# PEER gates on one Trainium2 core: a weight split in two parts, compares with one operand in PSUM, accumulators that hold their banks

## The chip, the cores and the metric

The kernel runs on one core of a Trainium2 chip. The metric is device time in microseconds; the median of three executions of the kernel before is 3694.65 us (3694.28 to 3696.64). The engines are PE (TensorE, matmuls; PEld is its weight load), DVE (VectorE), ACT (ScalarE), POOL (GpSimd) and SP (SyncE, which issues most transfers).

## The reference

Two model blocks run over 256 tokens of width 2048. The change touches only the PEER feed-forward part of the first block: eight heads pick 16 experts each out of 16384, by two lists of 128 keys.

```python
s1, i1 = lax.top_k(s[..., 0, :], PEER_TOPK)
s2, i2 = lax.top_k(s[..., 1, :], PEER_TOPK)
cand = s1[..., :, None] + s2[..., None, :]          # 16 x 16 per head
top_s, pos = lax.top_k(cand, PEER_TOPK)             # eid = i1 * 128 + i2
gate = jax.nn.softmax(top_s, axis=-1)
act = gelu(einsum('nd,nhkd->nhk', hx, expert_u[e]))
return einsum('nhk,nhkd->nd', gate * act, expert_v[e])
```

The kernel does not gather experts. It computes the activation of every expert for every token (up pass), a dense matrix of gates that is zero for experts not chosen, and multiplies the product of both into expert_v (down pass).

## The kernel before

float32 products are made from two float32r parts: a high part (a cast on ACT, L140) and a low part (x minus high, a subtraction on DVE or POOL, L142). `K.split` issues both. float32r operands take one matmul record; products of plain float32 operands take two.

**The up pass** (`Peer.up`, L1171) runs over 128 blocks of 128 experts. For a block it loads 1 MB of peer_u (tile `raw`, two buffers), transposes it with two DVE instructions (L1184, tile `tr`, four buffers), splits it in halves (tiles `hi` and `lo`, three buffers each) and issues 16 pairs of matmuls: 512 columns with the high part (L1203) and 256 columns with the low part (L1204). The block's accumulator `gu` is one PSUM bank from a pool of six that go round. Eviction is an ACT copy (L239), a DVE add (L241, tile `act`) and a Gelu on ACT (L1212).

**The side work** is put between the blocks. `Peer.route` (L1047) finds the 128 chosen pairs of keys for half of the tokens: maxima, sums of candidates (L1073), and a lookup by compare (L1099), multiply (L1101) and sum (L1103), all on DVE. `Peer.gates` (L1124) then builds the dense gates, four tokens at a time. The 128 choices of a token lie on the partitions. `factors` makes two matrices for each token: o2, one-hot in the second key (L1136, one compare of 512 elements for four tokens), and o1, one-hot in the first key times the weight. o1 comes from ACT by two activations (L1142, L1143: the square of the distance, then Relu of w minus w times that square) or from DVE by a tensor_scalar (L1145). GATE_ACT says for how many of the four tokens ACT does it: four in the first half of the tokens, two in the second. `product` multiplies the two by an fp32 matmul of 128 columns for each token (L1152) into a bank `psg`, and `store` copies the bank to SBUF on ACT (L1158).

**The order.** `UP_PLAN` (L30) gives the rate: 40 blocks beside the first half's route, 50 blocks beside the second half's route and the first half's gates in turn, 32 blocks beside the second half's gates; the last 6 blocks have no side work. From the 90th block on (`UP_FREE`, L31) DVE computes one of four low parts in every block, before that in every second block. Inside the block a scheduler (L2042) fixes the order of the instructions on each engine when the program is built. Engines work through their queues in that order.

Of the kernel before, what the change touches and what calls it, by code (L numbers as in the profile page):

```python
# [9 lines left out]
F32 = mybir.dt.float32  # L10
F32R = mybir.dt.float32r
# [3 lines left out]
AF = mybir.ActivationFunctionType  # L15
ALU = mybir.AluOpType
# [4 lines left out]
T = 256  # L21
# [10 lines left out]
GATE_ACT = (4, 2)  # L32
# [961 lines left out]
class Peer:  # L994
    def __init__(self, k, hn2, pool, h_d):
        self.k, self.hn2, self.pool, self.tr, self.h_d = k, hn2, pool, pool, h_d
        self.anchor = {}
        self.pI = [pool.tile([128, T], F32, name=f"pI{i}") for i in range(3)]
        self.ni1, self.nw = (pool.tile([128, T], F32, name=f"pN{i}") for i in range(2))
        self.iota = pool.tile([128, 128], F32, name="iota")  # L1000
        k.nc.gpsimd.iota(self.iota, pattern=[[1, 128]], base=0, channel_multiplier=0,
                         allow_small_or_imprecise_dtypes=True)
# [44 lines left out]
    def route(self, pool, tt):  # L1047

        k, nc, a = self.k, self.k.nc, self.k.a
# [3 lines left out]
        it16 = self.iota[:, 0:16]  # L1053
        sv = W("sv", [128, 16, 16])
# [11 lines left out]
        P.tensor_copy(sif, si)  # L1066
        tv = W("tv", [128, 8, 16])
# [3 lines left out]
        def sums(h):  # L1071
            cds[h] = W("cd", [128, 16, 16], 2)
            V.tensor_tensor(cds[h], sv[:, 2 * h, :, None].to_broadcast([128, 16, 16]),  # L1073
                            sv[:, 2 * h + 1, None, :].to_broadcast([128, 16, 16]), op=ALU.add)
# [41 lines left out]
        for i in range(3):  # L1116
            V.tensor_copy(self.pI[i][:, tt * 128:(tt + 1) * 128], ps[:, i * 128:(i + 1) * 128])
        for dst, i in ((self.ni1, 0), (self.nw, 2)):
            V.tensor_scalar(dst[:, tt * 128:(tt + 1) * 128], ps[:, i * 128:(i + 1) * 128], -1.0, None, op0=ALU.mult)
# [4 lines left out]
    def gates(self, tt, scr, g_d, act):  # L1124


        k, nc = self.k, self.k.nc
        i1, i2, w = self.pI
# [3 lines left out]
        key = self.iota[:, None, :].to_broadcast([128, 4, 128])  # L1132

        def factors(t0):
            o2 = self.pool.tile([128, 4, 128], F32, tag="oh2", bufs=3, name="oh2")
            nc.vector.tensor_tensor(o2, key, tok(i2, t0), op=ALU.is_equal)  # L1136
            o1 = self.pool.tile([128, 4, 128], F32, tag="oh1", bufs=3, name="oh1")
            for j in range(4):
                t = t0 + j
                if j < act:  # L1140

                    S.activation(o1[:, j], self.iota, AF.Square, bias=self.ni1[:, t:t + 1])  # L1142
                    S.activation(o1[:, j], o1[:, j], AF.Relu, scale=self.nw[:, t:t + 1], bias=w[:, t:t + 1])  # L1143
                else:
                    nc.vector.tensor_scalar(o1[:, j], self.iota, i1[:, t:t + 1], w[:, t:t + 1], op0=ALU.is_equal,  # L1145
                                            op1=ALU.mult)
            return t0, o2, o1

        def product(t0, o2, o1):
            ps = k.bank("psg")  # L1150
            for j in range(4):
                nc.tensor.matmul(ps[:, j * 128:(j + 1) * 128], lhsT=o2[:, j], rhs=o1[:, j], start=True, stop=True)  # L1152
            return t0, ps
# [10 lines left out]
        for t0 in range(128 * tt, 128 * tt + 136, 4):  # L1164
# [4 lines left out]
            yield  # L1169

    def up(self, act_d):  # L1171
# [24 lines left out]
        def back():  # L1196
            n, c, hi, lo = ready.pop(0)
            if c == 0:
                self.ps = k.gp.tile([128, 512], F32, tag="g", name="gu")
            ps = self.ps  # L1200
# [108 lines left out]
def peer(k, x2, xq, norm, hh, h_d, g_d, act_d, acts, es, finish):  # L1309
# [11 lines left out]
    with tc.tile_pool(name="up", bufs=1) as up:  # L1321
        pe.pool = up
        main = pe.up(act_d)
        route = [pe.route(up, tt) for tt in range(2)]
        gates = [pe.gates(tt, two, g_d, act) for tt, act in enumerate(GATE_ACT)]
# [754 lines left out]
```

## Time and profile before

| | us |
|---|---|
| median of three executions | 3694.65 |
| the profiled execution | 3696.7 |
| its span | 3694.9 |
| PE busy in the span | 3570.3 (97%) |
| DVE busy | 2617.8 (71%) |
| ACT busy | 2030.2 (55%) |
| POOL busy | 1323.9 (36%) |

The up pass lies between about 999 and 1836 us. Gate products stand between 1253.8 and 1790.2 us. Shares over the whole span say little about it, since stages with other limits are in them; the stretches of the pass are read one by one below. Busy time of PE is modelled and overlaps; the distance between the starts of two matmuls says more than their durations.

### The profile page before, as it was taken

The page shows a single profiled execution, that of the slowest core. Times are in us where ns is not written, and L with a number is a line of the kernel's source. Part 1 is how long each engine was busy: PE and PEld are TensorE (multiplying, and loading weights), DVE is VectorE, ACT ScalarE, POOL GpSimd, SP SyncE. Part 2 cuts the span into 40 slices and gives each one's busy share as a digit, 9 for nine tenths or more (in the row PEclk, how much of TensorE's full clock was granted, in tenths as well). Part 3 has the DMA queues.
Part 4 walks back from the last instruction along what each step waited for, and adds up shares of the span by engine and source line. Part 5 has one row for each costly group of instructions (what it writes and reads, how often), then busy time and mean ns, then how long its engine had stood idle before and what let it go on. Part 6 is the DMA issues. An engine that isn't in the chain of part 4 may idle for free.

```text
span 3694.9 us, 55970 instructions
## 1 busy us (share of the span) xinstructions
PE 3570.3 (97%) x19751; PEld 2991.5 (81%) x19751; DVE 2617.8 (71%) x4165; ACT 2030.2 (55%) x3861; POOL 1323.9 (36%) x1339
## 2 busy tenths in 40 slices
PE   9999999999999999998899999999999999989998
PEld 7678888878888888887788888888788887878777
DVE  5766777667588888788644444446899879667766
ACT  5555556545454677766544444445555667444674
POOL 1333223211288777755511111111234544142001
PEclk9999999999999999999999999999999999999999
DMA  7444434477698888878977777765554445645434
GB/s 221 138 160 129 131 122 132 140 230 244 172 204 207 201 213 221 219 180 208 253 246 237 229 235 231 221 200 187 164 172 145 141 139 171 192 145 184 144 120 149
DMA packets 377277, 681.21 MB, mean 184 GB/s; under 512 B 44493, under 2 KB 128373, under 8 KB 375845
## 3 DMA queue, kind: packets, MB, share of 16 engines
q1 hardware_dynamic: 343104, 625.05, 58.0%
q10 hardware_dynamic: 33893, 52.58, 4.2%
q8 instruction: 156, 2.56, 0.3%
q14 instruction: 124, 1.02, 0.1%
HBM read 627.57 MB, written 47.22 MB: 183 GB/s over the span
## 4 chain that ended last, share of the span: by engine, by line
PE 45%; DVE 3%; ACT 1%; DMA 1%; issue 1%; POOL 0%; SPq 0%; ACTq 0%; DVEq 0%; POOLq 0%
PE g L205 13%; PE g L207 7%; PE gv L1250 5%; PE gv L1251 5%; PE gv L1252 5%; PE dv L1252 2%; PE dv L1250 2%; PE dv L1251 2%; DVE lo L142 1%; PE g L229 1%; PE g L228 1%; PE g L230 1%; ACT hi L140 1%; PE psl L1840 1%; DMA raw<-in_peer_u_dram 1%
## 5 line engine op out<-in xcount | busy, mean ns | idle before, releaser
L142 DVE TENSOR_TENSOR lo<-raw,hi 128x1024 fp32r<-128x1024 f32 (+3 forms) x856 | 1039.3, 1218 | 622.6 <-ACT hi L140 618.7
L140 ACT CAST hi<-raw 128x1024 fp32r<-128x1024 f32 (+3 forms) x858 | 867.3, 1013 | 908.3 <-PE gv L1252 395.8
L205 PE MATMUL g<-x,hi 128*128 128x512 f32 x3040 | 1091.2, 401 | 13.0 <-DVE x L1662 9.0
L207 PE MATMUL g<-x,lo 128*128 128x256 f32 x3040 | 844.0, 288 | 16.7 <-DVE lo L142 16.5
L1203 PE MATMUL gu<-x,hi 128*128 128x512 f32 x2048 | 733.0, 398 | 1.7 <-ACT hi L140 1.7
L142 POOL TENSOR_TENSOR lo<-tr,hi 128x512 fp32r<-128x512 f32 x429 | 589.2, 1401 | 250.8 <-ACT hi L140 175.2
L205 PEld LDWEIGHTS g<-x,hi 128*128 128x128 f32 x3040 | 568.3, 189 | 133.0 <-issue 19.8
L207 PEld LDWEIGHTS g<-x,lo 128*128 128x128 f32 x3040 | 575.0, 189 | 53.0 <-DVE lo L142 26.9
L1204 PE MATMUL gu<-x,lo 128*128 128x256 f32 x2048 | 580.2, 284 | 30.4 <-POOL lo L142 27.3
L1203 PEld LDWEIGHTS gu<-x,hi 128*128 128x128 f32 x2048 | 386.4, 189 | 88.6 <-ACT hi L140 2.4
L1204 PEld LDWEIGHTS gu<-x,lo 128*128 128x128 f32 x2048 | 386.7, 189 | 48.5 <-POOL lo L142 44.7
L1184 DVE STREAM_TRANSPOSE tr<-raw 128x1024 f32<-128x1024 f32 x256 | 309.0, 1231 | 90.6 <-POOL lo L142 43.8
L140 ACT CAST hi<-tr 128x512 fp32r<-128x512 f32 x512 | 290.0, 616 | 76.2 <-PE gu L1203 54.5
L142 POOL TENSOR_TENSOR g<-scr,g 128x512 fp32r<-128x512 f32 x64 | 114.9, 1797 | 572.0 <-ACT g L140 572.0
L1252 PE MATMUL gv<-hi,g 128*128 128x512 f32 x756 | 299.7, 396 | 0.0
L1251 PE MATMUL gv<-lo,g 128*128 128x512 f32 x756 | 299.7, 396 | 0.0
L1250 PE MATMUL gv<-hi,g 128*128 128x512 f32 x756 | 238.4, 396 | 0.0
L1212 ACT ACTIVATE act<-act 128x256 f32<-128x256 f32 x128 | 53.4, 417 | 222.6 <-DVE act L241 222.3
L205 PE MATMUL g<-y2m,hi 128*128 128x512 f32 x512 | 175.2, 397 | 0.3 <-ACT hi L140 0.3
L1251 PEld LDWEIGHTS gv<-lo,g 128*128 128x128 f32 x756 | 142.4, 188 | 34.7
L1252 PEld LDWEIGHTS gv<-hi,g 128*128 128x128 f32 x756 | 142.4, 188 | 34.7
L1250 PEld LDWEIGHTS gv<-hi,g 128*128 128x128 f32 x756 | 142.4, 188 | 34.7
(604 smaller groups left out, 5856.4 us busy)
## 6 DMA issues: line engine op xcount, KB each, us to landing
raw<-in_peer_u_dram SPq DMA_DIRECT2D x512, 256.0 KB
raw<-in_peer_v_dram SPq DMA_DIRECT2D x256, 512.0 KB
raw<-in_a_w_in_dram SPq DMA_DIRECT2D x160, 512.0 KB
raw<-in_w_in_dram SPq DMA_DIRECT2D x136, 512.0 KB
raw<-in_b_w_in_dram SPq DMA_DIRECT2D x64, 512.0 KB
raw<-in_a_w_out_dram SPq DMA_DIRECT2D x48, 512.0 KB
raw<-in_w_out_dram SPq DMA_DIRECT2D x32, 512.0 KB
raw<-in_w_peer_query_dram SPq DMA_DIRECT2D x32, 512.0 KB
```

The source lines that it names most:

```text
L140: ins = nc.scalar.copy(hi, x) if heng == "act" else nc.vector.tensor_copy(hi, x)
L142: return ins, eng.tensor_tensor(lo, x, hi.bitcast(F32), op=ALU.subtract)
L205: nc.tensor.matmul(ps[f], lhsT=hi[:, k, f * 128:(f + 1) * 128], rhs=x2[:, q, :], start=(q == 0), stop=False)
L207: nc.tensor.matmul(ps[f][:, 0:T], lhsT=lo[:, k, f * 128:(f + 1) * 128], rhs=x2[:, q, 0:T], start=False, stop=(q == nk - 1))
L228: nc.tensor.matmul(ps[tt], lhsT=x, rhs=w, start=(q == 0), stop=False)
L1184: st["t"] = nc.vector.transpose(tr.rearrange("p b (u j) -> p u b j", u=2), raw[:, 2 * u:2 * u + 2].rearrange("p u (b j) -> p u b j", j=32))
L1203: nc.tensor.matmul(ps, lhsT=hi[:, j], rhs=self.hn2[:, q, :], start=(q == 0), stop=False)
L1204: st["m"] = nc.tensor.matmul(ps[:, 0:T], lhsT=lo[:, j], rhs=self.hn2[:, q, 0:T], start=False, stop=(q == KT - 1))
L1212: nc.scalar.activation(o, o, AF.Gelu)
L1250: nc.tensor.matmul(p, lhsT=x, rhs=hi, start=first, stop=False)
L1251: nc.tensor.matmul(p, lhsT=x, rhs=lo, start=False, stop=False)
L1252: nc.tensor.matmul(p, lhsT=g2[:, T + tt * 128:T + tt * 128 + 128], rhs=hi, start=False, stop=last)
```

## The change

`gates` no longer uses ACT for o1. Each token's weight is split into a high and a low float32r part (`pw`, made once for each half by `K.split`), and one scalar_tensor_tensor on DVE makes both parts of o1 for a token: 256 elements, the compare of the key with i1, times the two weights. o2 and o1 are float32r tiles, and each token takes two matmuls of 128 columns, one for each part, that accumulate. The key list iota is copied into a PSUM bank, and sv and sif (the route's values and indices) are copied into PSUM as well, so that the compares and the route's three operations read one operand from PSUM and one from SBUF. `banks` takes all six banks of the pool for the whole pass: four accumulators that go round by block number, one bank for iota and sif, one for sv.

```diff
--- before.py
+++ after.py
@@ -29,7 +29,6 @@
 LAST = [(1536, 2), (1792, 2)]
 UP_PLAN = (40, 50, 32)
 UP_FREE = 90
-GATE_ACT = (4, 2)
 DECAY_C = math.exp(-0.5)
 HALVES = [slice(0, 64), slice(64, 128)]
 QUAD = "(a b i)"
@@ -995,8 +994,8 @@
     def __init__(self, k, hn2, pool, h_d):
         self.k, self.hn2, self.pool, self.tr, self.h_d = k, hn2, pool, pool, h_d
         self.anchor = {}
-        self.pI = [pool.tile([128, T], F32, name=f"pI{i}") for i in range(3)]
-        self.ni1, self.nw = (pool.tile([128, T], F32, name=f"pN{i}") for i in range(2))
+        self.pI = [pool.tile([128, T], F32, name=f"pI{i}") for i in range(2)]
+        self.pw = pool.tile([128, 2, T], F32R, name="pw")
         self.iota = pool.tile([128, 128], F32, name="iota")
         k.nc.gpsimd.iota(self.iota, pattern=[[1, 128]], base=0, channel_multiplier=0,
                          allow_small_or_imprecise_dtypes=True)
@@ -1050,7 +1049,7 @@
         V, S, P, E = nc.vector, nc.scalar, nc.gpsimd, nc.tensor
         s = self.s
         W = lambda n, shape, bufs=1, dt=F32, p=pool: p.tile(shape, dt, tag="w_" + n, bufs=bufs, name=n)
-        it16 = self.iota[:, 0:16]
+        it16 = self.iotaP[:, 0:16]
         sv = W("sv", [128, 16, 16])
         si = W("si", [128, 16, 16], dt=U32)
         for j in range(16):
@@ -1064,13 +1063,16 @@
                 yield
         sif = W("sif", [128, 16, 16])
         P.tensor_copy(sif, si)
+        S.copy(self.sifP, sif)
+        S.copy(self.svP, sv)
+        sif, svP = self.sifP, self.svP
         tv = W("tv", [128, 8, 16])
         ti = W("ti", [128, 8, 16], dt=U32)
         cds = {}
 
         def sums(h):
             cds[h] = W("cd", [128, 16, 16], 2)
-            V.tensor_tensor(cds[h], sv[:, 2 * h, :, None].to_broadcast([128, 16, 16]),
+            V.tensor_tensor(cds[h], svP[:, 2 * h, :, None].to_broadcast([128, 16, 16]),
                             sv[:, 2 * h + 1, None, :].to_broadcast([128, 16, 16]), op=ALU.add)
 
         sums(0)
@@ -1113,43 +1115,39 @@
         ps = k.bank("psr")
         for i in range(3):
             E.transpose(ps[:, i * 128:(i + 1) * 128], res[:, i].rearrange("p h j -> p (h j)"), k.ident)
-        for i in range(3):
-            V.tensor_copy(self.pI[i][:, tt * 128:(tt + 1) * 128], ps[:, i * 128:(i + 1) * 128])
-        for dst, i in ((self.ni1, 0), (self.nw, 2)):
-            V.tensor_scalar(dst[:, tt * 128:(tt + 1) * 128], ps[:, i * 128:(i + 1) * 128], -1.0, None, op0=ALU.mult)
+        ts = slice(tt * 128, (tt + 1) * 128)
+        for i in range(2):
+            V.tensor_copy(self.pI[i][:, ts], ps[:, i * 128:(i + 1) * 128])
+        k.split(ps[:, 256:384], self.pw[:, 0, ts], self.pw[:, 1, ts])
         yield
 
     GATE_TOK = 32
 
-    def gates(self, tt, scr, g_d, act):
-
+    def gates(self, tt, scr, g_d):
 
         k, nc = self.k, self.k.nc
-        i1, i2, w = self.pI
+        (i1, i2), w = self.pI, self.pw.bitcast(F32)
         S = nc.scalar
         n = self.GATE_TOK
         tok = lambda x, t: x[:, t:t + 4, None].to_broadcast([128, 4, 128])
-        key = self.iota[:, None, :].to_broadcast([128, 4, 128])
+        key = lambda n: self.iotaP[:, None, :].to_broadcast([128, n, 128])
 
         def factors(t0):
-            o2 = self.pool.tile([128, 4, 128], F32, tag="oh2", bufs=3, name="oh2")
-            nc.vector.tensor_tensor(o2, key, tok(i2, t0), op=ALU.is_equal)
-            o1 = self.pool.tile([128, 4, 128], F32, tag="oh1", bufs=3, name="oh1")
+            o2 = self.pool.tile([128, 4, 128], F32R, tag="oh2", bufs=3, name="oh2")
+            nc.vector.tensor_tensor(o2, key(4), tok(i2, t0), op=ALU.is_equal)
+            o1 = self.pool.tile([128, 4, 2, 128], F32R, tag="oh1", bufs=3, name="oh1")
             for j in range(4):
                 t = t0 + j
-                if j < act:
-
-                    S.activation(o1[:, j], self.iota, AF.Square, bias=self.ni1[:, t:t + 1])
-                    S.activation(o1[:, j], o1[:, j], AF.Relu, scale=self.nw[:, t:t + 1], bias=w[:, t:t + 1])
-                else:
-                    nc.vector.tensor_scalar(o1[:, j], self.iota, i1[:, t:t + 1], w[:, t:t + 1], op0=ALU.is_equal,
-                                            op1=ALU.mult)
+                nc.vector.scalar_tensor_tensor(o1[:, j], key(2), i1[:, t:t + 1], w[:, :, t:t + 1].to_broadcast([128, 2, 128]),
+                                               op0=ALU.is_equal, op1=ALU.mult)
             return t0, o2, o1
 
         def product(t0, o2, o1):
             ps = k.bank("psg")
             for j in range(4):
-                nc.tensor.matmul(ps[:, j * 128:(j + 1) * 128], lhsT=o2[:, j], rhs=o1[:, j], start=True, stop=True)
+                for u in range(2):
+                    nc.tensor.matmul(ps[:, j * 128:(j + 1) * 128], lhsT=o2[:, j], rhs=o1[:, j, u], start=(u == 0),
+                                     stop=(u == 1))
             return t0, ps
 
         def store(t0, ps):
@@ -1167,6 +1165,15 @@
             done = product(*made) if made else None
             made = factors(t0) if t0 < 128 * tt + 128 else None
             yield
+
+    def banks(self):
+
+
+        b = [self.k.gp.tile([128, 512], F32, tag="g", name="gu") for _ in range(6)]
+        self.acc = b[0:4]
+        self.iotaP = b[4][:, 0:128]
+        self.sifP, self.svP = (x.rearrange("p (j i) -> p j i", j=16) for x in (b[4][:, 256:512], b[5][:, 0:256]))
+        self.k.nc.scalar.copy(self.iotaP, self.iota)
 
     def up(self, act_d):
 
@@ -1195,9 +1202,7 @@
 
         def back():
             n, c, hi, lo = ready.pop(0)
-            if c == 0:
-                self.ps = k.gp.tile([128, 512], F32, tag="g", name="gu")
-            ps = self.ps
+            ps = self.acc[n % 4]
             for j in range(8):
                 q = c * 8 + j
                 nc.tensor.matmul(ps, lhsT=hi[:, j], rhs=self.hn2[:, q, :], start=(q == 0), stop=False)
@@ -1320,9 +1325,10 @@
     two = scr.rearrange("p (a b) f -> p a (b f)", a=2)
     with tc.tile_pool(name="up", bufs=1) as up:
         pe.pool = up
+        pe.banks()
         main = pe.up(act_d)
         route = [pe.route(up, tt) for tt in range(2)]
-        gates = [pe.gates(tt, two, g_d, act) for tt, act in enumerate(GATE_ACT)]
+        gates = [pe.gates(tt, two, g_d) for tt in range(2)]
         side = pe.anchored(itertools.chain(route[0], alternate(route[1], gates[0]), gates[1]))
         R, G, due = pe.ROUTE_STEPS, 34, 0.0
         rates = [R / UP_PLAN[0]] * UP_PLAN[0] + [(R + G) / UP_PLAN[1]] * UP_PLAN[1] + [G / UP_PLAN[2]] * UP_PLAN[2]
```

The instructions outside the up pass stand as before, and POOL's and SP's order is the same throughout. On ACT, beside the second half's gates, the kernel before has the Gelu (L1212) ahead of two casts (L140), and activations for o1 between the casts:

```order
L239 COPY half<-gu 128x256
L1212 ACTIVATE act<-act 128x256
L140 CAST hi<-tr 128x8x64 x2
L1142 ACTIVATE oh_18264<-iota,pN_9354 128x128 x2
L1158 COPY scr<-psg 128x128x4
L1143 ACTIVATE oh_18264<-oh_18264,pI_9353,pN_9355 128x128 x2
L140 CAST hi<-tr 128x8x64 x2
L239 COPY half<-gu 128x256
```

In the same place of the changed program (its lines are one to five numbers off) the copy of the accumulator is L238, the casts are L139, the Gelu is L1217 and the copy of the gate bank is L1156:

```order
L238 COPY half<-gu 128x256
L139 CAST hi<-tr 128x8x64 x2
L1217 ACTIVATE act<-act 128x256
L1156 COPY scr<-psg 128x128x4
L139 CAST hi<-tr 128x8x64 x2
L238 COPY half<-gu 128x256
```

The four activations are gone, and two casts now stand ahead of the Gelu.

On DVE, in the same part of the pass, before: the compare for o2 (L1136), two tensor_scalar for o1, the eviction's add (L241), the low part (L142), two transposes (L1184).

```order
L1136 TENSOR_TENSOR oh_18115<-iota,pI_9352 128x512
L1145 TENSOR_SCALAR oh_18117<-iota,pI_9351,pI_9353 128x128 x2
L241 TENSOR_TENSOR act<-gu,half 128x256
L142 TENSOR_TENSOR lo<-tr,hi 128x8x64
L1184 STREAM_TRANSPOSE tr<-raw 128x2x16x32 x2
```

In the changed program (`gu` is here the bank with iota in L1137 and L1141, and an accumulator in L240):

```order
L1137 TENSOR_TENSOR oh_18053<-gu,pI_9352 128x512
L1141 SCALAR_TENSOR_TENSOR oh_18055<-gu,pI_9351,pw 128x256 x4
L240 TENSOR_TENSOR act<-gu,half 128x256
L141 TENSOR_TENSOR lo<-tr,hi 128x8x64
L1191 STREAM_TRANSPOSE tr<-raw 128x2x16x32 x2
```

Nothing changes places there; four instructions of 256 elements stand where two of 128 stood. In the second stretch, where ACT had made all of o1, the four are new on DVE.

On PE, a group of gate products between a block's pairs, before:

```order
L1203 MATMUL gu<-x_78,hi 128x512
L1204 MATMUL gu<-x_78,lo 128x256
L1152 MATMUL psg<-oh_17823,oh_17821 128x128 x4
L1203 MATMUL gu<-x_78,hi 128x512
L1204 MATMUL gu<-x_78,lo 128x256
```

and in the changed program:

```order
L1208 MATMUL gu<-x_78,hi 128x512
L1209 MATMUL gu<-x_78,lo 128x256
L1149 MATMUL psg<-oh_17757,oh_17755 128x128 x8
L1208 MATMUL gu<-x_78,hi 128x512
L1209 MATMUL gu<-x_78,lo 128x256
```

Eight matmuls stand in the place of four; some groups stand a few pairs earlier or later than before.

## Rows read from the trace of the kernel before

**Rows 1.** The page's first line.

```profile
span 3694.9 us, 55970 instructions
```

**Rows 2.** Stretches: length, busy PE PEld DVE ACT POOL (xinstructions), PEclk, DMA share, GB/s.

```profile
995.00:1240.00 245.00, 239.28 (x1343) 205.62 (x1342) 200.41 (x414) 123.16 (x256) 196.17 (x149) 0.99 0.87 201
1240.00:1560.00 320.00, 317.58 (x1896) 278.57 (x1895) 279.06 (x467) 248.10 (x600) 246.39 (x180) 1.00 0.88 215
1560.00:1795.00 235.00, 213.55 (x1252) 181.97 (x1251) 196.08 (x223) 145.50 (x347) 130.72 (x94) 0.99 0.78 192
```

**Rows 3.** Groups, 1240 to 1560 us: busy us, mean ns | idle before, releaser.

```profile
L1203 PE MATMUL gu<-x,hi 128*128 128x512 f32 x819 | 291.4, 397 | 0.0
...
L1136 DVE TENSOR_TENSOR oh<-iota,pI 128x512 f32<-128x512 f32 x32 | 35.5, 1109 | 0.0
...
L1101 DVE TENSOR_TENSOR oh<-oh,sif 128x256 f32<-128x256 f32 x16 | 17.3, 1080 | 0.0
L1099 DVE TENSOR_TENSOR oh<-abf,iota 128x256 f32<-128x256 f32 x16 | 12.9, 805 | 0.0
L1073 DVE TENSOR_TENSOR cd<-sv 128x256 f32<-128x256 f32 x8 | 7.6, 946 | 0.0
```

**Rows 4.** Groups, 1560 to 1795 us.

```profile
L1203 PE MATMUL gu<-x,hi 128*128 128x512 f32 x498 | 180.7, 400 | 0.0
...
L1136 DVE TENSOR_TENSOR oh<-iota,pI 128x512 f32<-128x512 f32 x32 | 48.1, 1507 | 0.0
L1145 DVE TENSOR_SCALAR oh<-iota,pI,pI 128x128 f32<-128x128 f32 x64 | 42.7, 709 | 0.0
...
L142 DVE TENSOR_TENSOR lo<-tr,hi 128x512 fp32r<-128x512 f32 x31 | 23.3, 753 | 30.9 <-ACT hi L140 30.8
```

**Rows 5.** Chain of waits, one turn near 1765 us: start, us, what.

```profile
1764.81 0.34 DVE act L241
...
1765.50 0.61 ACT hi L140
...
1766.13 0.70 DVE lo L142
...
1766.92 2.40 DVE tr L1184 x2
...
1772.37 0.34 DVE act L241
```

**Rows 6.** Timeline of ACT: start, us, instruction, idle before and its releaser.

```profile
1741.94 0.42 ACT L1212 ACTIVATE act<-act 128x256 f32<-128x256 f32 x1 [2.97 <-DVE act L241]
```

**Rows 7.** Timeline of PE, a group of gate products (records).

```profile
1492.40 0.39 PE L1203 MATMUL gu<-x,hi 128*128 128x512 f32 x1
1492.63 0.28 PE L1204 MATMUL gu<-x,lo 128*128 128x256 f32 x1
1492.74 1.05 PE L1152 MATMUL psg<-oh,oh 128*128 128x128 f32 x8
1493.55 0.48 PE L1203 MATMUL gu<-x,hi 128*128 128x512 f32 x1
1493.87 0.28 PE L1204 MATMUL gu<-x,lo 128*128 128x256 f32 x1
```

**Rows 8.** Timeline of PE, four fp32 products of 64 columns (eight records).

```profile
280.02 1.00 PE L596 MATMUL psW<-U,Q 128*128 128x64 f32 x8
280.82 0.36 PE L207 MATMUL g<-x,lo 128*128 128x256 f32 x1
```

**Rows 9.** Single lines of DVE: xcount, min/median/max ns, first and last start, forms.

```profile
L352 DVE SCALAR_TENSOR_TENSOR x<-xt,par,x x16: 473/479/485, 7.2 to 36.3; 128x256 fp32r<-128x256 f32 x16
...
L2024 DVE TENSOR_TENSOR hh<-dT,hx x8: 673/678/692, 2556.8 to 2575.5; 128x512 f32<-128x512 f32 x8
...
L241 DVE TENSOR_TENSOR act<-gu,half x128: 378/410/425, 1024.6 to 1839.1; 128x256 f32<-128x256 f32 x128
...
L1099 DVE TENSOR_TENSOR oh<-abf,iota x32: 374/383/1516, 1122.9 to 1531.9; 128x256 f32<-128x256 f32 x32
```

## The prediction

> **What bounds the kernel now.** I read the page's span first [rows 1], then the table of stretches over the up pass, the only stage that the change touches [rows 2]. It falls into three stretches: route of the first token half (995 to 1240 us), route of the second half beside the first gates (1240 to 1560), and the second gates (1560 to 1795). The reader should see three different limits. In the first and second, TensorE is busy 239.3 of 245 and 317.6 of 320 us, so it sets the pace. In the third it is busy 213.6 of 235 only, and DVE is not full either (196.1).
>
> What one block of 128 experts costs comes from the groups by line. A block is 16 pairs of a 512-column and a 256-column matmul; 819 pairs in the second stretch [rows 3] are 51.2 blocks, so 320/51.2 = 6.25 us each; 498 pairs in the third [rows 4] are 31.1 blocks, so 7.55 us each. The PE timeline [rows 7] gives the floor: a pair takes 0.23 + 0.12 = 0.35 us, so a block 5.6 us, and a group of four gate products pushes the next pairs back by 0.90 us (without the group the next pair would have started at 1492.74 and its 256-column half at 1492.97; that half starts at 1493.87). Each stretch has 32 groups, one for each compare of L1136 [rows 3, 4]. The floor is therefore 51.2 × 5.6 + 32 × 0.90 = 315.5 us of the second stretch's 320, and 31.1 × 5.6 + 28.8 = 203 us of the third's 235: 4.5 us lost there, 32 us lost here.
>
> The chain of waits shows what takes those 32 us [rows 5]: one turn of 7.56 us, from the add at 1764.81 to the next at 1772.37, runs almost wholly through DVE: add, then a wait until ACT's cast at 1765.50, the low part, two transposes, the compare, two more compares. ACT's part in it is an order, not a load: in the timeline [rows 6] ACT stood 2.97 us waiting for DVE's add to run its Gelu, and the casts that DVE needs next stand behind that Gelu. Two things stretch DVE's own work: the compare of 512 elements takes 1507 ns and those of 128 elements 709 ns [rows 4].
>
> **The change part by part.** *Compares from PSUM.* The nearest rows with one operand in PSUM and one in SBUF are L2024 (128x512, 678 ns) and L241 (128x256, 410 ns, never above 425 in 128 runs although POOL was busy for most of that pass) [rows 9]. With both in SBUF the same shapes took 1109 and 1507 ns, 1080, 805 and 946 ns in the pass, while L1099 alone can do 374 [rows 3, 4, 9]. So the wait beside POOL goes, and I price the new forms by the PSUM rows. [...]
>
> *Second operand of the product.* Per group, four scalar_tensor_tensor of 256 elements come in. The nearest row is L352, the same operation with PSUM in, a scalar column and an SBUF operand: 479 ns [rows 9]. The bounds are that row and 1080 ns, the 256-element operation that contended [rows 3]; I take 479. Out go two tensor_scalar per group in the third stretch, and ACT's two activations for each token that it served: all four of a group in the second stretch, two in the third.
>
> DVE in the second stretch: compares 35.5 to 32 × 0.678 = 21.7; L1101, L1099 and L1073 from 37.8 to 40 × 0.410 = 16.4; 128 new ones × 0.479 = 61.3 come in. 279.1 − 13.8 − 21.4 + 61.3 = 305 us, against a TensorE floor of 315.5. In the third: 196.1 − (48.1 − 21.7) − 42.7 + 128 × 0.479 = 188 us, 6.05 per block, against TensorE's 203/31.1 = 6.53. DVE stays under TensorE in both, closely in the second.
>
> *The products.* Eight matmuls of 128 columns replace four fp32 ones (eight records). Streaming alone would be cheap: 512 columns take 0.23 and 256 take 0.12 us, so 128 would take 0.055 and a group 0.44. But fp32 products with 64 columns [rows 8] take as long as those with 128: eight records push the next matmul out by 0.80 us there, by 0.81 here [rows 7]. What does not shrink with the columns is the loading of 128 x 128 weights before every record, 0.11 us each; the new products load eight times too. I take 0.90 us per group, unchanged. The bounds are 0.44 and, if a narrow product of this type costs what an fp32 product costs (0.90/4 = 0.225 us each), 1.80. [...]
>
> *Order.* ACT loses four activations per group in the third stretch, and in the new order the two casts stand ahead of the Gelu, so that DVE's low part no longer waits behind DVE's own add: the 1.0 us between the add's end (1765.15) and the low part (1766.13) leaves the chain [rows 5]. What is late next is TensorE itself.
>
> *The rest.* Small copies into PSUM (one of iota, four for sv and sif), the weight's split and two evictions fewer per half: an estimated 0.4 us each by L241 of the same size [rows 9], on ACT and DVE, beside matmuls, and one-off. If that cover fails, some 3 us in all. The four accumulators turn once in four blocks, over 20 us, while one is evicted within a block, so holding the banks adds no wait. DMA moves what it moved; at 6.6 us a block the third stretch needs 192 × 235/207 = 218 GB/s, which the second stretch already had (215) [rows 2]. The first stretch stays at TensorE's pace.
>
> **The sum.** Third stretch: 6.53 plus the second's own loss of 4.5/51.2 = 0.09 per block is 6.62, times 31.1 is 206: −29 us. Second stretch: floor unchanged, DVE at 95% of it may cost a little: +2. Together −27 us from the profiled execution's 3696.7, which lies 2 us above the median of the runs shown: 3670 by the profile, 3668 by the median. The likeliest case's own range: third stretch 6.53 to 6.9 per block (−32 to −20), second −4 to +8, so 3657 to 3683.
>
> **Rivals.** (1) Narrow products at full price. The place is the group of eight in TensorE's queue; the price is 1.80 instead of 0.90 us, 64 times. Third stretch: 5.6 + 1.03 × 1.80 + 0.09 = 7.54 per block, no gain; second: +29 us, so 3724, slower. It decides from about 1.32 us a group on, where 64 × 0.42 eats the 27. For it: no row of the trace has this type of matmul with under 256 columns. Against: from 256 to 512 columns each of its matmuls takes only 0.11 us more, and each is one record, where the four fp32 products are eight [rows 7]. (2) Cheap products. With 0.44 us a group TensorE's floor in the third stretch is 6.05, level with DVE; 6.2 per block gives −42, the second stretch, then DVE's at about 310, −10: 3643. If half of the load hides, 0.67 a group, −37 and −8: 3651. [...] Against it are the 64-column records [rows 8]. (3) DVE becomes the bound. If it keeps all its present idle time (320 − 279 = 41 and 235 − 196 = 39 us), the second stretch takes 346 and the third 227: +18, 3713. For it: 95% busy in order. Against: much of that idle is waiting for a TensorE-paced loop, and the chain's wait for ACT goes. (4) The new scalar_tensor_tensor waits beside POOL like the old compares: 0.6 × 256 = 154 us more on DVE, 382 of 320 and 265 of 235: +90, 3785. Against: L241 [rows 9].
>
> **How the numbers follow.** Likeliest 0.60, cheap products 0.13, DVE the bound 0.09, full price 0.15, contention 0.03. The range, 3642 to 3716, runs from just under the cheap case to just over the DVE case and leaves out full price and contention. A measurement of this kernel tells 0.2% (7.4 us) from no change. Faster, under 3687: the first two cases but for a tail of 0.01, so 0.72. Within 0.2%: that tail and a mild form of the DVE case (0.05), 0.06. Slower: its full form (0.04), full price and contention, 0.22.
>
> **What would show it.** Right: in the third stretch blocks of about 6.6 us, TensorE busy as in the second, no wait of DVE's low part on ACT; scalar_tensor_tensor near 480 ns, the compare near 680; eight gate products pushing the next pair out by 0.9 us. Wrong: product groups at 1.3 us or more, or TensorE waiting on the second operand (DVE) or on low parts in the second stretch with DVE over 97% busy; then the time is not below the old.

## The result, and the profile after

The changed kernel takes 3655.84 us (median of four, 3653.99 to 3660.67) against 3694.47 for the one before: a ratio of 0.9897, 95% interval 0.9880 to 0.9914. The prediction was 3668, range 3642 to 3716.

The up pass cut at the same four marks in each kernel, from the start of its first accumulating matmul: the end of the first half's route (its last psr transpose), the end of the second half's, the last gate product, the last accumulating matmul of the high part. Stretch lengths in us, one profiled execution each:

| kernel | first | second | third | tail | pass |
|---|---|---|---|---|---|
| before | 239.4 | 318.7 | 232.7 | 46.2 | 837.0 |
| changed | 236.2 | 313.9 | 202.8 | 45.1 | 798.0 |
| difference | -3.2 | -4.8 | -29.9 | -1.1 | -39.0 |

What comes after the pass took 1858.5 us before and 1861.5 in this execution of the changed kernel, 1856.4 in another, so nothing outside the pass explains the gain.

The stretches of the changed kernel, second and third, answer to [rows 2]. Columns: window, its length, busy time of PE, PEld, DVE, ACT and POOL (instructions), TensorE's granted clock, DMA share, GB/s:

```profile
1235.50:1549.40 313.90, 313.90 (x1890) 277.45 (x1888) 284.28 (x593) 167.02 (x345) 227.68 (x179) 1.00 0.89 219
1549.40:1752.20 202.80, 201.27 (x1239) 178.58 (x1237) 183.35 (x287) 105.80 (x219) 121.39 (x93) 1.00 0.89 219
```

TensorE is busy in all of the second stretch and in 201.3 of 202.8 us of the third; DVE has 183 us to do there and no longer sets the pace. The chain of waits from 1715 to 1728 us, in the third stretch, is PE alone, where the turn of [rows 5] ran almost wholly through DVE. Over the whole third stretch (second line) PE has 90% of the chain and loads of peer_u have 5.9%:

```profile
by line: PE gu L1208 59.6%; PE gu L1209 29.0%; PE psg L1149 13.0%
by line: PE gu L1208 51.7%; PE gu L1209 26.3%; PE psg L1149 12.0%; DMA raw<-in_peer_u_dram 5.9%; DVE oh L1141 2.7%; DVE tr L1191 1.7%; DVE oh L1137 1.2%; issue 1.0%; DVE lo L141 1.0%; DVE act L240 0.2%; DVE pw L141 0.1%; DVEq L1191 0.0%
```

DVE's groups of the third stretch (line, operation, shapes, count; busy us, mean ns; idle before) answer to [rows 4]:

```profile
L1141 DVE SCALAR_TENSOR_TENSOR oh<-gu,pI,pw 128x256 fp32r<-128x256 f32 x128 | 52.5, 470 | 0.0
L141 DVE TENSOR_TENSOR lo<-tr,hi 128x512 fp32r<-128x512 f32 x31 | 33.7, 1086 | 2.6 <-ACT hi L139 2.6
L1137 DVE TENSOR_TENSOR oh<-gu,pI 128x512 fp32r<-128x512 f32 x32 | 20.9, 654 | 0.0
```

The compare takes 654 ns, where it took 1507; the new scalar_tensor_tensor 470. DVE's low part waits 2.6 us for ACT in the whole stretch, where it waited 30.9. It has itself become slower (1086 ns, 753 before). Both of its operands still lie in SBUF, and the 15 of these 31 that take 1010 to 1692 ns each have a POOL instruction beside them for 0.46 us or more; the seven that have none take 676 to 683.

The timeline of TensorE around one group of products answers to [rows 7] (start, duration of the row):

```profile
1725.21 0.28 PE L1209 MATMUL gu<-x,lo 128*128 128x256 f32 x1
1725.33 1.00 PE L1149 MATMUL psg<-oh,oh 128*128 128x128 f32 x8
1726.17 0.44 PE L1208 MATMUL gu<-x,hi 128*128 128x512 f32 x1
1726.45 0.28 PE L1209 MATMUL gu<-x,lo 128*128 128x256 f32 x1
```

Without the group the next 256-column half would have started at 1725.21 + 0.35 = 1725.56; it starts at 1726.45. The group costs 0.89 us, and did 0.90.

### The profile page after: what moved, and what is told of

It is laid out like the page before. It is cut to its first block, busy times and chain, and to the rows that moved or that the text cites. A ratio compares the mean times of both kernels' runs of the same rounds, so it can differ in the third digit from the quotient of the medians.

```text
span 3658.8 us, 55713 instructions
## 1 busy us (share of the span) xinstructions
PE 3559.2 (97%) x19751; PEld 2995.4 (82%) x19751; DVE 2608.9 (71%) x4353; ACT 1912.6 (52%) x3484; POOL 1292.8 (35%) x1339
## 4 chain that ended last, share of the span: by engine, by line
PE 67%; DVE 6%; DMA 4%; issue 2%; ACT 1%; POOL 1%; SPq 0%; ACTq 0%; DVEq 0%; POOLq 0%
PE g L204 16%; PE gu L1208 10%; PE g L206 8%; PE gu L1209 5%; PE gv L1255 5%; PE gv L1256 5%; PE gv L1257 5%; DMA raw<-in_peer_u_dram 2%; PE dv L1257 2%; PE dv L1255 2%; PE dv L1256 2%; DVE lo L141 2%; PE psg L1149 1%; DVE tr L1191 1%; ACT hi L139 1%
## 5 line engine op out<-in xcount | busy, mean ns | idle before, releaser
L139 ACT CAST hi<-raw 128x1024 fp32r<-128x1024 f32 (+3 forms) x858 | 867.2, 1013 | 917.4 <-PE gv L1257 393.0
L141 POOL TENSOR_TENSOR lo<-tr,hi 128x512 fp32r<-128x512 f32 x429 | 555.4, 1320 | 245.7 <-ACT hi L139 207.0
L139 ACT CAST hi<-tr 128x512 fp32r<-128x512 f32 x512 | 290.8, 617 | 199.2 <-PE gu L1208 165.7
L1217 ACT ACTIVATE act<-act 128x256 f32<-128x256 f32 x128 | 53.5, 418 | 174.9 <-DVE act L240 174.0
```

The source lines that it names most:

```text
L139: ins = nc.scalar.copy(hi, x) if heng == "act" else nc.vector.tensor_copy(hi, x)
L141: return ins, eng.tensor_tensor(lo, x, hi.bitcast(F32), op=ALU.subtract)
L1217: nc.scalar.activation(o, o, AF.Gelu)
```

## The experiments

The edits are shown shortened. Each ratio is to the kernel before, measured beside the run; its medians lie between 3694.03 and 3696.64 us.

**PSUM operands alone (ps_only).** The changed kernel with the second operand, the products and with them ACT's order put back; the banks stay held:

```diff
-  nc.vector.scalar_tensor_tensor(o1[:, j], key(2), ...)
+  if j < act:
+      S.activation(o1[:, j], self.iota, AF.Square, bias=...)
+      S.activation(o1[:, j], o1[:, j], AF.Relu, scale=..., bias=...)
+  else:
+      nc.vector.tensor_scalar(o1[:, j], self.iota, i1[...], w[...], ...)
-  for u in range(2): nc.tensor.matmul(..., rhs=o1[:, j, u], ...)
+  nc.tensor.matmul(..., rhs=o1[:, j], start=True, stop=True)
```

> The kernel before, with one part of the change: banks held, iota, sif and sv read from PSUM by the 512-element compare and by the three operations of route. The second operand of the product is made as before (ACT's two activations, DVE's tensor_scalar from SBUF), the products are fp32, and ACT's list still has the Gelu ahead of the casts in the third stretch. Theory of the prediction: the compare is 0.83 us shorter in each of 32 turns of the third stretch, so its block falls from 7.55 to about 6.7 us (208 us of 235), while ACT's link of 1.0 us stays in the loop; 3660 to 3670. Rival, ACT's relief is what counts (order and activations): no gain, 3685 to 3697. Rival, the PSUM operand alone is what counts: as the changed kernel, 3653 to 3660.

Measured: 3663.95 us (3661.10 to 3668.69), ratio 0.9916 (0.9902 to 0.9929); stretches 235.6, 314.0, 213.1. Most of the gain, and all of it in the first two stretches, comes with the operands in PSUM (of the compare and of route's three operations). In the third stretch 10 us are missing. DVE's groups there:

```profile
L1147 DVE TENSOR_SCALAR oh<-iota,pI,pI 128x128 f32<-128x128 f32 x64 | 49.9, 822 | 0.0
L142 DVE TENSOR_TENSOR lo<-tr,hi 128x512 fp32r<-128x512 f32 x31 | 22.6, 728 | 31.0 <-ACT hi L140 30.9
L1139 DVE TENSOR_TENSOR oh<-gu,pI 128x512 f32<-128x512 f32 x32 | 20.8, 656 | 0.0
```

The tensor_scalars, still from SBUF, rose from 709 to 822 ns, and the low part still waits 31 us for ACT.

**All operands from SBUF (sb_all).**

```diff
-  it16 = self.iotaP[:, 0:16]      key = ... self.iotaP ...      svP, sif = copies in PSUM
+  it16 = self.iota[:, 0:16]       key = ... self.iota ...       svP, sif = sv, sif
```

> The changed kernel with every operand back in SBUF (iota, sif, sv), banks still held, split and products as changed, ACT's list in the new order. Theory of the prediction: without the PSUM operand DVE's work contends with POOL again. If scalar_tensor_tensor of 256 elements then takes the 1.08 us of the old 256-element compare, DVE has about 393 us to do in the second stretch (315 now) and 286 in the third (205 now): about 3815, far slower than before. If it does not contend but the compares do, DVE has 315 and 208: about 3675. Rival, ACT's relief is what counts and PSUM nothing: 3653 to 3662.

Measured: 3743.70 us (3741.36 to 3746.45), ratio 1.0130 (1.0113 to 1.0146): slower than before. The rival (ACT's relief is enough) is out: ACT is as free here as in the changed kernel. The time lies between the two cases named for the theory: some of the scalar_tensor_tensors wait, not all. Stretches:

```profile
1239.50:1605.60 366.10, 328.55 (x1888) 279.78 (x1887) 353.26 (x596) 161.93 (x344) 243.85 (x179) 0.99 0.75 186
1605.60:1840.90 235.30, 217.32 (x1239) 184.52 (x1237) 223.26 (x286) 102.60 (x218) 128.51 (x92) 0.96 0.76 188
```

DVE is busy 353 of 366 and 223 of 235 us: it is the bound. One line of the source view (count, then minimum/median/maximum in ns) shows how, first of this kernel, then of the changed one:

```profile
L1141 DVE SCALAR_TENSOR_TENSOR oh<-iota,pI,pw x256: 467/473/1593, 1245.3 to 1832.5; 128x256 fp32r<-128x256 f32 x128
```

```profile
L1141 DVE SCALAR_TENSOR_TENSOR oh<-gu,pI,pw x256: 453/471/484, 1240.8 to 1741.9; 128x256 fp32r<-128x256 f32 x128
```

The same instruction takes 470 ns or, beside POOL, up to 1593; with one operand in PSUM it is never above 484 in 256 runs. What it meets is POOL's subtraction. Counted over the trace of sb_all, 167 of the 256 have no POOL instruction beside them and take 467 to 479 ns; 79 take 872 to 1593, and each of these overlaps a POOL instruction. In the changed kernel 204 of the 256 overlap one, and none is longer for it. In the timelines of DVE and of POOL (start, duration, count), four of them take 4.78 us while POOL runs its low parts until 1503.48; in POOL's pause the 256-element operations of L1101 and L1103 then take 0.41 us each:

```profile
1499.38 4.78 DVE L1141 SCALAR_TENSOR_TENSOR oh<-iota,pI,pw 128x256 fp32r<-128x256 f32 x4
1504.08 0.41 DVE L1101 TENSOR_TENSOR oh<-abf,iota 128x256 f32<-128x256 f32 x1
...
1505.07 0.41 DVE L1103 TENSOR_TENSOR oh<-oh,sif 128x256 f32<-128x256 f32 x1
```

```profile
1497.56 5.92 POOL L141 TENSOR_TENSOR lo<-tr,hi 128x512 fp32r<-128x512 f32 x4
1506.19 2.52 POOL L141 TENSOR_TENSOR lo<-tr,hi 128x512 fp32r<-128x512 f32 x2 [2.71 <-ACT hi L139]
```

Rival (4) of the prediction priced the waiting of the scalar_tensor_tensors alone at +90 us. Here they wait and so do the compares, and the whole costs +50: the forecast had all 256 of them wait, and 79 did. The split needs the PSUM operand. The first stretch, where only route's three operations differ, is 238.6 us here and 236.2 in the changed kernel: route's operands are worth 2.4 us of the 3.2 gained there. The banks are held in both, so holding them is not the gain.

**No split (fp32_one).**

```diff
-  nc.vector.scalar_tensor_tensor(o1[:, j], key(2), ...)         # 256 elements
+  nc.vector.tensor_scalar(o1[:, j], self.iotaP, i1[...], w[...], ...)   # 128, fp32
-  for u in range(2): nc.tensor.matmul(..., rhs=o1[:, j, u], ...)
+  nc.tensor.matmul(..., rhs=o1[:, j], start=True, stop=True)    # fp32, two records
```

> The changed kernel without the split in two parts: the weight stays fp32, the second operand is one tensor_scalar of 128 elements from PSUM per token, and the product is one fp32 matmul per token as before (two records each). ACT makes none of it. Theory of the prediction: eight weight loads set the group either way, TensorE paces the pass, so the time stays, 3652 to 3660, though DVE has some 0.2 us per token less to do (about 50 us). Rival, the single-pass products make the group cheaper: the group grows by 0.2 us or more, 64 times, 3669 or more.

Measured: 3651.46 us (3648.05 to 3656.28), ratio 0.9884 (0.9869 to 0.9899); stretches 236.1, 313.8, 201.0, 43.3. Neither the split nor the single-pass products bring anything. It was run again beside the changed kernel:

> The kernel of fp32_one again, beside the changed kernel in the same session. By the theory that TensorE paces the pass it is level with it or up to 4 us below (DVE has 28 us less to do and TensorE waited 11 us in the changed kernel's pass): 3649 to 3655.

> The changed kernel again, for the comparison with fp32_one in the same session: 3653 to 3659.

Measured: 3650.27 us (3648.95 to 3651.83; ratio 0.9872, 0.9857 to 0.9887) against 3656.84 (3654.76 to 3661.70; 0.9895, 0.9879 to 0.9910). The plain version lies 6.6 us below the changed one and no run of the two overlaps, but the intervals do. It leaves nothing out of the computation.

**One product per token (hi_only).** The low part's product is left out.

```diff
-  for u in range(2): nc.tensor.matmul(..., rhs=o1[:, j, u], start=(u == 0), stop=(u == 1))
+  nc.tensor.matmul(..., rhs=o1[:, j, 0], start=True, stop=True)
```

> The changed kernel with the low part's product left out (one single-pass product per token; the second operand is still made whole). Theory of the prediction: the group has four weight loads, about 0.43 us instead of 0.85, and TensorE paces the pass, so 64 x 0.42 = 27 us go, 3629, if DVE (279 of 302 us and 181 of 192 us then) lets it; 3627 to 3640. Rival, the group is not bound by its loads, or another engine has become the bound of the pass: 3648 to 3658.

Measured: 3651.96 us (3647.88 to 3654.61), ratio 0.9880 (0.9863 to 0.9896). The group did halve: in TensorE's timeline the next pair starts 0.39 us after the group's first record, not 0.84.

```profile
1703.04 0.28 PE L1207 MATMUL gu<-x,lo 128*128 128x256 f32 x1
1703.16 0.56 PE L1148 MATMUL psg<-oh,oh 128*128 128x128 f32 x4
1703.55 0.45 PE L1206 MATMUL gu<-x,hi 128*128 128x512 f32 x1
1703.84 0.28 PE L1207 MATMUL gu<-x,lo 128*128 128x256 f32 x1
```

Yet 4 us came of the 27 expected: the second stretch took 314.3 us, the third 196.6. So another bound lies close behind TensorE's. The next three runs ask what sets the group, and what that bound is.

**Half the columns (cols64).**

```diff
-  nc.tensor.matmul(ps[:, j*128:(j+1)*128], rhs=o1[:, j, u], start=(u == 0), stop=(u == 1))
+  nc.tensor.matmul(ps[:, j*128+u*64:j*128+u*64+64], rhs=o1[:, j, u, u*64:u*64+64], start=True, stop=True)
```

> The changed kernel with eight products of 64 columns per group in place of eight of 128 (the high part makes the first half of the keys, the low part the second; half of the sum is left out). Theory of the prediction, weight loads set the group: it pushes the next pairs out by 0.84 us as before, 3653 to 3659. Rival, columns set it (hi_only halved both columns and loads, to 0.40 us a group): 0.40 to 0.45 us a group, and the time as hi_only's, 3648 to 3654.

Measured: 3653.83 us (3652.47 to 3655.92), ratio 0.9884 (0.9869 to 0.9899). The time lies in the ranges of both, so TensorE's timeline decides. The next pair starts 0.81 us after eight records of 64 columns began, 0.84 after eight of 128. By the reading of the section on the result, how much later the next 256-column half starts, both groups cost 0.89 us (1703.58 + 0.35 = 1703.93, and it starts at 1704.82), and hi_only's cost 0.45 (1703.04 + 0.35 = 1703.39, and it starts at 1703.84). So the records count, and not their columns.

```profile
1703.58 0.28 PE L1210 MATMUL gu<-x,lo 128*128 128x256 f32 x1
1703.70 0.97 PE L1150 MATMUL psg<-oh,oh 128*128 128x64 f32 x8
1704.51 0.47 PE L1209 MATMUL gu<-x,hi 128*128 128x512 f32 x1
1704.82 0.28 PE L1210 MATMUL gu<-x,lo 128*128 128x256 f32 x1
```

The changed kernel's second stretch has 1890 matmul records and 1888 weight loads, so about one for each. In its timeline a load is a row of 0.19 us, and the eight loads of a group, overlapping, take 0.97, so that one starts (0.97 - 0.19)/7 = 0.11 us after the other:

```profile
1725.22 0.97 PEld L1149 LDWEIGHTS psg<-oh,oh 128*128 128x128 f32 x8
1726.11 0.19 PEld L1208 LDWEIGHTS gu<-x,hi 128*128 128x128 f32 x1
```

That fits the loads as what sets the group. Another fixed cost of a record is not told apart from its load: no run has one without the other.

**What is behind TensorE (hi_ts, hi_ts_raw3).**

```diff
-  nc.vector.scalar_tensor_tensor(o1[:, j], key(2), ...)
+  nc.vector.tensor_scalar(o1[:, j], self.iotaP, i1[...], w[...], ...)   # 128, float32r
   # hi_ts_raw3: every third block loads into a third raw tile
```

> What paces the pass once the products are halved (hi_only gained 4 us of 27). One single-pass product per token, and the second operand is one tensor_scalar of 128 elements from PSUM in place of a scalar_tensor_tensor of 256 (the low part of the weight is left out). Theory 1, DVE (281 of 314 us in hi_only's second stretch, 182 of 197 in its third): with 10 and 16 us less on it the second stretch falls to 302 to 308 and the third to 190 to 194: 3632 to 3645. Theory 2, the loads of peer_u through two raw buffers (DVE's transposes waited 38 us for them in hi_only, 21 in the changed kernel): no gain over hi_only, 3648 to 3655.

> As hi_ts, with a third raw buffer for the loads of peer_u in this pass. Theory 2 (two buffers pace the pass): the transposes' wait for the loads goes and TensorE's floor of 27 us less shows, 3627 to 3638. Theory 1 (DVE): the same as hi_ts. If the loads' rate itself is the bound and not the buffers (DMA share 0.88 to 0.91): within 4 us of hi_ts as well, with DMA share above 0.9 and the transposes still waiting for loads.

Measured: hi_ts 3634.78 us (3632.35 to 3635.36), ratio 0.9831 (0.9818 to 0.9845); hi_ts_raw3 3635.95 (3630.61 to 3640.40), 0.9833. It was DVE: with some 16 us less on it in the third stretch (182.1 to 166.0) TensorE's saving shows.

```profile
1234.90:1536.10 301.20, 300.53 (x1762) 263.52 (x1761) 270.22 (x591) 166.57 (x344) 227.21 (x179) 1.00 0.91 228
1536.10:1726.90 190.80, 187.63 (x1108) 163.73 (x1107) 166.03 (x286) 102.98 (x214) 118.74 (x92) 1.00 0.92 230
```

```profile
1243.80:1543.90 300.10, 300.10 (x1762) 263.50 (x1761) 271.16 (x583) 167.37 (x344) 226.93 (x178) 1.00 0.93 228
1543.90:1729.60 185.70, 185.70 (x1108) 163.69 (x1107) 177.84 (x286) 104.76 (x214) 119.89 (x92) 1.00 0.97 236
```

The third buffer shortens the third stretch by 5 us more, to TensorE's full floor (185.7 of 185.7), but what it saves is not in the time: in that execution the first stretch took 247.7 us, where hi_ts took 235.8. Of these 12 us TensorE stands 9.1 in one wait, from 1017 to 1026 us, for a cast on ACT, ahead of which the transposes waited 7.0 us for their load of peer_u; what held that load back is open. Both leave out the low part of the weight; they are the fastest of these kernels, but their gates are made from one float32r part.

**ACT's order.** The prediction counted as a step of its own that the casts come ahead of the Gelu. The first try to undo it, old_order:

```diff
+  late = k.tc.issue_after(st["g"].ins) if c and "g" in st else nullcontext()
+  with late:                       # casts of a second half, behind the newest Gelu
     st["h"], st["l"] = k.split(...)
```

> The changed kernel with ACT's list put back into the old order: the two casts behind each Gelu are held until that Gelu is issued. Nothing else is changed; ACT has 106 of 205 us to do in the third stretch. Theory of the prediction: the order costs, since DVE's low part again waits for ACT, which waits for DVE's add; the third stretch goes from 203 us to about 213, as in the run that kept the order (ps_only), the second stays at TensorE's floor: 3662 to 3672. Rival, it was the activations' time on ACT and not the order: 3653 to 3659.

Measured: 3802.88 us (3796.87 to 3804.61), ratio 1.0285 (1.0270 to 1.0299). The edit missed its aim: it tied the casts, in every stretch, to the Gelu of one block before, where the old order had that of two blocks before and in the third stretch alone. ACT's copy then stood 268 us waiting for TensorE's block to end:

```profile
ACT half L238 <- PE gu L1211: 268.1, 82, 5.5
```

It says nothing of the old order. Two edits that change the order alone follow, one on each kernel.

The order alone, on the kernel before (order_only):

```diff
-  nc.scalar.activation(o, o, AF.Gelu)        # in back(), with its store
+  late.append((n, o, self.act))              # blocks 90 to 121: issued after split(n + 2, 1)
```

> The kernel before with one thing changed: in blocks 90 to 121 ACT's list has the Gelu of a block behind the casts of the block after the next, as the changed kernel's list has it, and not ahead of them. Compares, second operands and products as before. Theory of the prediction: the link of 1.0 us between DVE's add and its low part leaves the loop, 7.56 - 1.0 = 6.56 us a block, the third stretch 233 to 205..212: 3670 to 3680. Rival, DVE's waiting compares pace the loop and the order alone changes little: 3688 to 3697.

Measured: 3688.99 us (3684.82 to 3695.97), ratio 0.9977 (0.9966 to 0.9987). By the medians that is 7.65 us less than the kernel before; in the profiled execution, the slowest of the eight, the third stretch is 227.9 us, 4.8 less than before. The link did go, and paid little of the 21 to 28 us that the theory expected. DVE's groups in its third stretch, against 48.1 us (1507 ns), 42.7 (709) and an idle time of 30.9 in [rows 4]:

```profile
L1145 DVE TENSOR_SCALAR oh<-iota,pI,pI 128x128 f32<-128x128 f32 x64 | 65.6, 1066 | 0.0
L1136 DVE TENSOR_TENSOR oh<-iota,pI 128x512 f32<-128x512 f32 x32 | 51.1, 1601 | 0.0
L142 DVE TENSOR_TENSOR lo<-tr,hi 128x512 fp32r<-128x512 f32 x31 | 24.0, 776 | 1.2 <-ACT hi L140 1.0
```

The tensor_scalar's durations before, and in order_only (minimum/median/maximum):

```profile
L1145 DVE TENSOR_SCALAR oh<-iota,pI,pI x64: 332/335/1333, 1569.1 to 1779.6; 128x128 f32<-128x128 f32 x64
```

```profile
L1145 DVE TENSOR_SCALAR oh<-iota,pI,pI x64: 333/1295/1360, 1569.8 to 1776.5; 128x128 f32<-128x128 f32 x64
```

The same instruction takes 335 ns or about 1300. Why they changed stands in POOL's timeline, first of the kernel before, then of order_only:

```profile
1697.62 1.28 POOL L142 TENSOR_TENSOR lo<-tr,hi 128x512 fp32r<-128x512 f32 x1 [2.85 <-PE gu L1203]
1699.92 2.97 POOL L142 TENSOR_TENSOR lo<-tr,hi 128x512 fp32r<-128x512 f32 x2 [1.02 <-ACT hi L140]
```

```profile
1698.32 4.23 POOL L142 TENSOR_TENSOR lo<-tr,hi 128x512 fp32r<-128x512 f32 x3 [3.29 <-ACT hi L140]
```

DVE's two tensor_scalars of the same turn, before:

```profile
1701.68 1.55 DVE L1145 TENSOR_SCALAR oh<-iota,pI,pI 128x128 f32<-128x128 f32 x2
```

Before, the Gelu kept the casts of a block apart, and POOL's three low parts fell in two groups: one ran beside the transposes, two beside the compare and the first tensor_scalar, and the second tensor_scalar was free. With the casts together the three run in one row, to 1702.55, beside the compare and both tensor_scalars. In the third stretch 27 such rows of three stand where 27 single ones and 27 pairs stood. Of the 64 tensor_scalars, 37 had no POOL instruction beside them before (332 to 339 ns each) and 14 have none in order_only (333 to 338). Some 30 us of waiting became 26 us of longer instructions (22.9 on the tensor_scalars, 3.0 on the compares), and DVE is the bound of the stretch:

```profile
1559.10:1787.00 227.90, 208.92 (x1237) 179.81 (x1238) 218.76 (x226) 144.70 (x347) 128.96 (x93) 0.99 0.80 193
```

One turn of the loop in order_only's DVE timeline, where [rows 5] had the wait for ACT behind the add:

```profile
1695.03 0.41 DVE L241 TENSOR_TENSOR act<-gu,half 128x256 f32<-128x256 f32 x1
1695.37 0.68 DVE L142 TENSOR_TENSOR lo<-tr,hi 128x512 fp32r<-128x512 f32 x1
1696.13 2.37 DVE L1184 STREAM_TRANSPOSE tr<-raw 128x1024 f32<-128x1024 f32 x2
1698.43 1.74 DVE L1136 TENSOR_TENSOR oh<-iota,pI 128x512 f32<-128x512 f32 x1
1700.09 2.54 DVE L1145 TENSOR_SCALAR oh<-iota,pI,pI 128x128 f32<-128x128 f32 x2
1702.55 0.41 DVE L241 TENSOR_TENSOR act<-gu,half 128x256 f32<-128x256 f32 x1
```

No gap is left, and the turn still takes 7.52 us.

The old order on the changed kernel (old_order2):

```diff
+  held = c == 1 and 94 <= n < 124
+  with k.tc.issue_after(gelu[n - 2].ins) if held else nullcontext():
     st["h"], st["l"] = k.split(...)
```

> The changed kernel with the reverse edit, in blocks 94 to 123 alone: the casts of the second half of a block are held until the Gelu of two blocks before is issued, which is the order of the kernel before (old_order held them for the Gelu of one block before, which no kernel here had). Theory of the prediction: the loop has ACT's link again, 6.5 + some 0.3 us a block as in ps_only (213 of 203 us): 3662 to 3670. Rival, the order costs nothing once compares read PSUM: 3653 to 3659.

Measured: 3656.78 us (3653.32 to 3658.93), ratio 0.9890 (0.9875 to 0.9905); the third stretch 205.6 us, 2.8 more than in the changed kernel, whose time beside it (3656.84) is the same. The theory's 3662 to 3670 is missed. The wait came back in part, DVE's low part stands 10.7 us for ACT, but DVE has 178 of 205.6 us to do there and can wait.

| kernel | third stretch, us | operands | ACT's order |
|---|---|---|---|
| before | 232.7 | SBUF | old |
| order_only | 227.9 | SBUF | new |
| sb_all | 235.3 | SBUF, scalar_tensor_tensor | new |
| ps_only | 213.1 | compare in PSUM, tensor_scalar in SBUF | old |
| old_order2 | 205.6 | PSUM | old |
| changed | 202.8 | PSUM | new |
| fp32_one | 201.0 | PSUM, tensor_scalar | new |

## Why the prediction came out, and where its reasons did not

- **The time, 3668 forecast, 3655.84 measured.** It lies within the range, and just under the likeliest case's own 3657 to 3683 (by its terms, -32 and -4, that case begins at 3659). Of the 39 us that the pass gained, 27 were forecast.
- **Third stretch, 206 us forecast, 202.8 measured.** Right in size: TensorE's floor. It ends there because DVE's operations no longer wait beside POOL (the compare takes 641 to 681 ns, 643 to 1783 before); the table above shows it from both sides. One of the two reasons given for it, the order, was not needed: old_order2 is at 205.6 without it. That TensorE's floor holds with either order kept the number right; the forecast did not know it, so in this part it was lucky.
- **Compares from PSUM** at 0.678 and 0.410: 0.652 and, for route's three, 0.382 to 0.406 (medians). Right. That L241 took 410 ns with one operand in PSUM and L1099 374 with both in SBUF shows no price of the PSUM operand: L1101 of the kernel before, with both operands in SBUF, has 408 at its best.
- **scalar_tensor_tensor at 479 ns, no contention:** 453 to 484. Right. The sum of DVE was too high (305 forecast in the second stretch, 284 measured), mainly since 128 × 0.479 = 61.3 us took 52.9: four in a row take 1.64 us, each starting before the one ahead has ended. The low parts fell too, from 31.3 to 26.2 us. That left DVE further from TensorE than rival (3) feared.
- **The group unchanged at 0.90, set by weight loads:** 0.89. That columns do not set it is shown by cols64 (64 columns, 0.89), that it goes with the number of records by hi_only (four, 0.45); that the load is what a record costs fits the loads' starts 0.11 us apart and is not shown alone. Rivals (1) and (2) fall with it. From the group's first record to the next pair it is 0.84/8 = 0.105 and, in hi_only, 0.39/4 = 0.098 us a record, while the row of a single load is 0.19 us long.
- **Order: "the 1.0 us ... leaves the chain".** This step failed as a reason. Alone it is worth 4.8 us of the 30 in the stretch, 7.65 by the medians (order_only); undone it costs 2.8 in the stretch and nothing in the time (old_order2). The chain of before showed the wait truly, but a wait in a loop is not a price: the same list that ended it also moved POOL's low parts beside tensor_scalars that take 335 ns alone and up to 1360 beside them. The compare's 0.83 us per turn was the larger half, as ps_only shows (19.6 us). What the remaining 7.5 us between ps_only and old_order2 come from, the tensor_scalars that still read SBUF or the activations on ACT, no run here separates.
- **Second stretch +2, first 0:** measured -4.8 and -3.2; these 8 us and the 2 not lost are most of the 12 us by which the forecast was too high. The forecast kept the second stretch's own loss of 4.5 us as if it were fixed. It was TensorE waiting for POOL's low parts: its weight loads waited 6.9 us for them in the first stretch and 5.1 in the second before, 3.4 and nothing after, and POOL's low part is shorter now (1320 ns in the mean, 1401 before). The waits (in all, times, longest), the first two of the kernel before, the last of the changed one:

```profile
PEld gu L1204 <- POOL lo L142: 6.9, 12, 1.2
PEld gu L1204 <- POOL lo L142: 5.1, 9, 1.7
PEld gu L1209 <- POOL lo L141: 3.4, 6, 1.0
```

- **The same two stretches in ps_only,** 235.6 and 314.0 us, have all of this gain without the split. The price of 2 us for DVE near its bound did not come.
- **The split** was priced at no gain on TensorE. Right: fp32_one does without it and is no slower.

## What to carry to other kernels

When a profile shows one instruction with a minimum of 332 ns and a maximum of 1333, look at the spread before the mean: here the price was what ran beside it (332 to 339 ns in all 37 runs with no POOL instruction beside them), and taking a wait out of its loop turned some 30 us of waiting into 26 us of longer instructions. Moving one of two operands into PSUM removed that here at no cost in the compare (641 ns at best, 643 before; 681 at most, 1783 before), and ps_only kept four fifths of the gain with that alone. A small product here costs its records, 0.89/8 = 0.11 us each with the weight load, with 64 columns as with 128; splitting it into as many records as before was free for TensorE (0.89 us a group, 0.90 before) and brought nothing.

## What the runs showed of the hardware

- A two-tensor compare costs the same from PSUM when nothing disturbs it: for 512 elements 643 ns at best before (both operands in SBUF), 641 with one in PSUM; 374 and 380 ns for 256 elements.
- A difference does show in tensor_scalar of 128 elements: in the median 335 ns from SBUF (the kernel before; 332 to 339 undisturbed) and 400 from PSUM (fp32_one), never above 413 in 256 runs there:

```profile
L1139 DVE TENSOR_SCALAR oh<-gu,pI,pI x256: 383/400/413, 1237.0 to 1734.2; 128x128 f32<-128x128 f32 x128
```

What makes these 65 ns, and whether they grow with the number of elements, no run here shows.
- A scalar_tensor_tensor with one tensor in PSUM, one in SBUF and a scalar column in SBUF stayed within 453 to 484 ns, though POOL was busy for 228 of the second stretch's 314 us.
- The transposes, with one tensor in SBUF to read, took 1187 to 1248 ns in all 256 runs of the kernel before, although POOL's low parts stood beside them for 43.8 us of its third stretch alone.
